# S5 output products of a hybrid decoder layer, regrouped by the shape of the array they use, with the next pair's kernel products moved into the same slot

## The chip, the cores and the metric

The kernel runs on one core of one Trainium2 chip. Times are device microseconds (us) from the start to the end of one execution; lower is better. TensorE is called PE in the profile, VectorE DVE, ScalarE ACT, GpSimd POOL; SP is SyncE, which here only issues DMAs.

## What is computed

One decoder layer over 2048 tokens of width 1024, all in float32. The part that matters here is the S5 branch of the mixer: 32 groups of 16 channels, each with a complex diagonal state of 64.

```python
proj = x @ w_in + b_in
u, ca, cb, gs, gc = jnp.split(proj, SPLITS, axis=-1)
_, _, s_re, s_im = lax.associative_scan(_s5_combine, (a_re, a_im, bu_re, bu_im), axis=1)
y = (jnp.einsum('blgp,ghp->blgh', s_re, c_re) - jnp.einsum('blgp,ghp->blgh', s_im, c_im))
y = jax.nn.gelu(y + d_skip * u)
glu = y @ w_glu + b_glu
s_out = glu[..., :D_MODEL] * jax.nn.sigmoid(glu[..., D_MODEL:])
c_out = _conv_mixer(ca, cb, conv_w, conv_b, ln_c_g, ln_c_b, w_cout, b_cout)
merged = jax.nn.sigmoid(gs) * s_out + jax.nn.sigmoid(gc) * c_out
h = _layer_norm(ALPHA * x + merged @ w_out + b_out, ln1_g, ln1_b)
```

A two-level mixture of 32 SwiGLU experts and a second norm follow; the change does not touch them.

## The kernel before, in words

**The stage.** The large projection runs by column tiles of 128 (`run`, L311), each over four strips of 512 tokens. One strip of one tile is called a slot: 24 products of 128x128 by 128x512 in a split float32 (high by high, high by low, low by high). In the gate tiles 12 to 27 and the two before them, `s5_step` (L729) is called ahead of each slot's products and works on the S5 branch, one pair of groups in four slots, counted from `k = slot - base` with `i, q = divmod(k, 4)`. The state is handled in chunks of 16 tokens: within a chunk a Toeplitz kernel (tile `M0`), from chunk to chunk the scanned state (tile `sx`).

- q = 0: `s5_c(i-1)`, the outputs of the pair before; then, among the vector work of this slot, `s5_a(i)`: twelve DVE products and two copies that make `CA`, `AB` and the block-diagonal `BD`, and the loads of `ut` and `rc` on SP's queue.
- q = 1: `s5_k(i)`: four transposes of `AB` into PSUM (copied by ACT to `BT`), two products of `BD` with `CA` (the chunk kernel, `kt`). DVE finishes `kt` at L651, POOL writes it to DRAM (L652), and SP loads it back as `M0` (L655).
- q = 2: `s5_b(i)`: eight products by 64 columns of `BT`, the two groups by turns, into the two halves of PSUM's partitions.
- q = 3: DVE's rotation and scan of the state, into `sx`.

**The output products.** `s5_c` (L690) makes, for each of the two groups and each half of a chunk, one or two products of `M0` with `ut` (all 128 rows of the array: "whole") and two of `CA` with `sx`, whose 64 rows are the upper or lower half of the array, according to the group ("row halves"). Group 0 comes first, then group 1, so that whole products and row halves alternate: M, CA CA, M M, CA CA, for each group. Each group has its own PSUM tile from the pool `aux`, which has four banks. All these operands are plain float32, and one such product stands in the trace as two passes, each with a weight load.

**What orders the work.** Engines run their own queues in order. Vector work that depends on other engines is put on a list by slot (`later`, `due`, L303 to L309). Work in the background (`bg`: the 31-tap convolution `conv`, L528, then the norm over the channels `norms`, L745, then loads and splits of the output projection's weights) is let out by `fill` (L128) at the end of every slot, as long as an estimated clock of DVE stands 4 us behind an estimated clock of PE (`pe_cost`, L73; `dve_cost`, L65); a step that yields "wait" ends the slot's turn. DVE's clock is never let fall more than 9 us behind. After the gate tiles comes the stage of the S5 output projection (L935 to L968), again 32 slots of 24 products; at its tile 7, strip 0, `drain(1)` (L951) lets out what is left of `norms` at once.

```python
V.t = max(V.t, PE.t + lead - SLOT)      # fill, lead = -4, SLOT = 5
while bg and V.t < PE.t + lead:
```

Of the kernel before, what the change touches and what calls it, by code (L numbers as in the profile page):

```python
# [23 lines left out]
D = 1024  # L24
NS = 4            # strips of 512 tokens
NT = 16           # tiles of 128 tokens
NE = 32
FF = 256
ALPHA = 2.0 ** 0.25
EPS = 1e-5  # L30
CAP = 2048        # rows of the dispatch table for one expert
JB = 4            # blocks of 128 rows laid out for each expert
MAGIC = 12582912.0
# [6 lines left out]

BASE, LEAD, SLOT = 0.10, -4.0, 5.0       # of the estimate of the vector engine's clock

# [12 lines left out]
class Clocked:  # L55
    """An engine whose instructions add their estimated length to a clock."""

# [19 lines left out]
def pe_cost(name, args, kw):  # L77
    if name == "transpose":
        return 0.107
    n = max(_free(args[2]), 64)  # L80
    return n / 2400.0 * (4 if args[2].dtype == F32 else 1)


@with_exitstack
def layer(ctx, tc, a, out, dbg=None):
# [28 lines left out]

    # ---------------------------------------------------------------- constants
    ident = cst.tile([128, 128], F32, name="ident")
# [7 lines left out]

    # vector work that fills the time which the matrix products leave
    bg = []
    ahead = []         # products for that work, at the start of the next slot

# [26 lines left out]

    # ---------------------------------------------------------------- helpers
    def split(hi, lo, src, src2=None):
# [17 lines left out]
    def wload(parts, nk):  # L175
        """parts: [(dram 2-d [rows, 128], first k)]"""
        w = Wt()
        w.nk = nk
        w.raw = wp.tile([128, nk, 128], F32, name="wraw", tag="raw", bufs=1, padded_shape=[128, 8, 128])
        for src, k0 in parts:  # L180
            n = src.shape[0] // 128
            SP.dma_start(w.raw[:, k0:k0 + n, :], src.rearrange("(k p) c -> p k c", p=128))
        return w
# [30 lines left out]

    # ---------------------------------------------------------------- x, transposed and split
    XH = [bigt([128, 8, 512], F32R, f"xh{s}") for s in range(NS)]
# [38 lines left out]
    xfetch(1)  # L255
    TILES = [8, 4, 9, 5, 10, 6, 0, 1, 2, 3, 11, 7] + list(range(12, 28))   # column tiles of w_in, in order
    WL = [(win, m) for m in TILES] + [(wglu, m) for m in range(8)] + [(wcout, m) for m in range(8)]
    WQ = {0: win(TILES[0])}

    def weights(n, s):  # L260
        """the next column tile's weights, while those of tile n are in use"""
        if n + 1 < len(WL):
            if s == 0:
                WQ[n + 1] = WL[n + 1][0](WL[n + 1][1])
            if s == 2:
                wsplit(WQ[n + 1])
# [32 lines left out]

    late = []          # (slot, f): vector work whose operands other engines have made by then  # L300
    slot = [0]
# [9 lines left out]
    def run(n, evac, between=None, first=None):  # L311
        """one column tile of w_in: the products, the next tile's weights, the work of the other engines"""
        w = WQ[n]
# [25 lines left out]

    # ---------------------------------------------------------------- S5: constants  # L340
    sp = spx.enter_context(tc.tile_pool(name="sp", bufs=1))
# [184 lines left out]

    # ---------------------------------------------------------------- convolution branch, u
    def conv(j):  # L528
# [21 lines left out]
    def xnext(s, k):  # L550
        # the next strip of x between the products of this one
        i = 4 * (s + 1) + k // 2
        if i < NT:
            if k % 2 == 0 and i == 4:
                xfetch(4)
                xfetch(5)
            if k % 2 == 0 and i + 2 < NT:
                xfetch(i + 2)
            xturn(i, k % 2)
        if (s, k) == (0, 7):  # L560
            biases()
# [31 lines left out]

    # ---------------------------------------------------------------- S5: one pair of groups at a time
    ss = sax.enter_context(tc.tile_pool(name="ss", bufs=1, side="right"))
    ST = {}

    def s5_a(i):
# [24 lines left out]
        for par in range(2):  # L623
            V.tensor_copy(bd[64 * par:64 * par + 64, :, 16 * par:16 * par + 16],
                          BB[64 * par:64 * par + 64, i])
        ut = ss.tile([128, 2, 2, 128], F32, name="utl", bufs=1)
        SP.dma_start(ut.rearrange("p g k c -> p (g k) c"),
# [62 lines left out]
    def s5_c(i):  # L690
        st = ST.pop(i)
        for par in range(2):
            g = 2 * i + par
            py = paux([128, 2, 128])
            q = slice(64 * par, 64 * par + 64)
            for mt in range(2):
                o = py[:, mt, :]
                PE.matmul(o, st.M0[:, par, 128 * mt:128 * mt + 128], st.ut[:, par, 1, :], start=True, stop=False)
                if mt:
                    PE.matmul(o, st.M0[:, par, 0:128], st.ut[:, par, 0, :], start=False, stop=False)  # L700
                for ri in range(2):
                    PE.matmul(o, st.CA[q, ri, 1 + 8 * mt:9 + 8 * mt, :].rearrange("p d h -> p (d h)"),
                              st.sx[q, ri, 0:128], start=False, stop=ri == 1)
            y1 = ss.tile([128, 2, 128], F32, name="y1", bufs=2)
# [15 lines left out]

    # ---------------------------------------------------------------- gates, with the S5 pairs between
    def g_evac(m):
# [5 lines left out]

    def s5_step():  # L729
        k = slot[0] - base  # L730
        if k == -1:
# [4 lines left out]
        if q == 0:  # L736
            if 1 <= i <= 16:
                s5_c(i - 1)
            if 1 <= i < 16:
                later(0, lambda: s5_a(i))  # L740
        elif i < 16 and q < 3:
            (None, s5_k, s5_b)[q](i)

    # ---------------------------------------------------------------- convolution branch: norm over the channels, silu
    def norms():  # L745
# [123 lines left out]

    # ---------------------------------------------------------------- S5 output, gated  # L870
    gx = ExitStack()
# [14 lines left out]
    def routing_constants():  # L886
        # what routing needs, and a table of dispatch without entries
        G.memset(wr, 0.0)
# [29 lines left out]
    def wo_second():  # L918
        # the output projection's weights, as far as there is room
        wo_load(2, gp, "xr", bufs=2)  # L920
# [48 lines left out]

    # ---------------------------------------------------------------- convolution branch, gated  # L970
    MH = {}
# [7 lines left out]

    # the last column tiles leave the first strips early, whose room the output projection's weights take  # L980
    ENDS = {(7, 1): 4, (6, 2): 5, (6, 3): 6, (7, 2): 7}
# [28 lines left out]

    # ---------------------------------------------------------------- output projection, norm, routing
    dx = ExitStack()
# [94 lines left out]
    def route1(p):  # L1107
# [9 lines left out]
        V.tensor_copy(gi, i8[:, :, 0:1])  # L1117
        # exp(d) = sigmoid(d) / sigmoid(-d)
        sp_, sm_ = small("r_sp", [2, 4]), small("r_sm", [2, 4])
# [60 lines left out]

    # ---------------------------------------------------------------- weights of the experts
    wg, wu, wd = a["w_gate"][0], a["w_up"][0], a["w_down"][0]
# [16 lines left out]

    # the split of one expert's weights, in six steps  # L1200
    def parts(i, k):
# [29 lines left out]
    for p in range(NP):  # L1231
        # the products of pair p, the norm of pair p - 1, the routing of pairs p - 1 and p - 2
        ta, tb = 2 * p, 2 * p + 1
# [69 lines left out]

    # ---------------------------------------------------------------- experts
    ex = ExitStack()
# [88 lines left out]
    def unit(e, b):  # L1394
        """block b of expert e, whose rows are turned; the last block's down projection is left to the next expert"""
        i, j = (e + b) % 2, e % 2
# [41 lines left out]

    # the rows of each expert's last block, and those of the block before it in the order of work
    lst = ep.tile([1, 64], I32, name="lst")  # L1440
# [49 lines left out]

    # rows beyond JB blocks of one expert
    mx = nc.values_load(cnt[0:1, NE:NE + 1], engines=ALL, min_val=0, max_val=S)
# [19 lines left out]

    # ---------------------------------------------------------------- second norm
    fp = ctx.enter_context(tc.tile_pool(name="fp", bufs=1, side="right"))
# [35 lines left out]

    POOL = {1: 1, 2: 3, 3: 1, 4: 3}          # one tile of these groups on the pool engine
    # in PSUM, so that no vector operation reads two tensors of SBUF beside the pool engine
    psx.close()
# [45 lines left out]
    def weave(work, r):  # L1599
        # the root of one group between the passes over others  # L1600
        while work:
# [42 lines left out]
```

## Time and profile before

| | |
|---|---|
| runs shown | 1890.2, 1893.34, 1894.98 us; median 1893.34 |
| profiled execution | span 1892.8 us from the first to the last instruction; no other time of this execution is given, and the median of the runs is 0.5 us above it |
| PE busy | 1755.2 us, 93% |
| DVE busy | 1316.6 us, 70% |
| ACT busy | 684.5 us, 36% |
| POOL busy | 300.9 us, 16% |
| S5 pairs, first to last output product | 285.4 to about 742 us |

A busy PE is not a PE at its best: matmuls overlap one another, and a product that starts late still covers the time. So the distance between the starts of products is read here, not the busy share.

### The profile page before, as it was taken

The numbers are of one execution on the slowest core, as the hardware profiler recorded it, in microseconds if no ns is written. First come the engines' busy times: TensorE is split into PE (matmuls) and PEld (weight loads), VectorE is DVE, ScalarE is ACT, GpSimd is POOL, SyncE is SP. The second block draws the span as 40 slices with busy tenths as digits, with TensorE's granted clock in tenths as the row PEclk, the third lists the DMA queues.
The fourth block names the chain that finished last, engine by engine and source line by source line (L and its number), as shares of the span: only waits on it lengthen the run. The fifth ranks groups of instructions, "written<-read, shape, count | busy, mean of one in ns | idle before, by whom it ended". The sixth has DMA issues, their size and how long they took to land. (4 is left out here: it accounts for less than half of the span.)

```text
span 1892.8 us, 24420 instructions
## 1 busy us (share of the span) xinstructions
PE 1755.2 (93%) x8328; PEld 1413.8 (75%) x8329; DVE 1316.6 (70%) x2388; ACT 684.5 (36%) x1047; POOL 300.9 (16%) x318
## 2 busy tenths in 40 slices
PE   8999999999999999999999999993899999999940
PEld 7888877777777777778888888883688787877730
DVE  5798798788888664664365768786666646657648
ACT  5101212222221234533130122223666656657654
POOL 2000001110101101000000011123223332233215
PEclk9999999999999999999999999996899999999975
DMA  7322422432422432534254333646989968899855
GB/s 221 82 90 61 118 65 75 137 95 75 138 74 92 131 121 91 193 119 156 80 192 128 117 112 114 175 118 191 274 264 287 277 179 249 264 270 291 252 172 230
DMA packets 235908, 301.47 MB, mean 159 GB/s; under 512 B 51230, under 2 KB 181360, under 8 KB 233152
## 3 DMA queue, kind: packets, MB, share of 16 engines
q1 hardware_dynamic: 192336, 212.47, 35.9%
q0 software_dynamic: 23008, 56.06, 10.8%
q10 hardware_dynamic: 20368, 30.42, 4.8%
q8 instruction: 112, 1.84, 0.4%
q14 instruction: 84, 0.69, 0.1%
HBM read 224.35 MB, written 92.31 MB: 167 GB/s over the span
## 5 line engine op out<-in xcount | busy, mean ns | idle before, releaser
L66 PE MATMUL mm<-xh,whi 128*128 128x512 f32 x896 | 362.7, 405 | 0.0
L66 PE MATMUL mm<-xl,whi 128*128 128x512 f32 x896 | 353.2, 394 | 0.0
L66 PE MATMUL mm<-xh,wlo 128*128 128x512 f32 x896 | 352.7, 394 | 0.0
L66 DVE SCALAR_TENSOR_TENSOR cvw<-cvw,cw 128x1024 f32<-128x1024 f32 x240 | 292.0, 1275 | 0.0
L66 PE MATMUL pg<-egu,bh 128*128 128x512 f32 x784 | 251.5, 402 | 5.3 <-ACT edn L1214 5.2
L66 PEld LDWEIGHTS mm<-xh,whi 128*128 128x128 f32 x896 | 168.6, 188 | 47.2 <-issue 8.2
L66 PEld LDWEIGHTS mm<-xh,wlo 128*128 128x128 f32 x896 | 168.5, 188 | 40.5
L66 PEld LDWEIGHTS mm<-xl,whi 128*128 128x128 f32 x896 | 169.0, 189 | 36.1 <-issue 0.7
L66 PEld LDWEIGHTS pg<-egu,bh 128*128 128x128 f32 x784 | 145.1, 190 | 38.2 <-ACT edn L1214 7.3
L66 DVE TENSOR_TENSOR egu<-eraw,egu 128x1024 fp32r<-128x1024 f32 x128 | 151.0, 1221 | 27.3 <-ACT egu L1214 21.5
L66 PE MATMUL mm<-wo,mh 128*128 128x512 f32 x512 | 165.3, 404 | 0.0
L66 PE MATMUL mm<-yt,whi 128*128 128x512 f32 x512 | 163.0, 399 | 2.1 <-ACT yt L848 1.5
L66 PE MATMUL pg<-egu,bl 128*128 128x512 f32 x392 | 155.3, 396 | 0.1
L725 ACT ACTIVATE gt<-mm,cols 128x512 f32<-128x512 f32 x64 | 44.0, 687 | 294.6 <-PE mm L66 282.4
L66 PE MATMUL pd<-edn,hh 128*128 128x512 f32 x392 | 130.1, 414 | 2.0 <-ACT yy L1390 1.1
L1214 ACT ACTIVATE egu<-eraw 128x1024 fp32r<-128x1024 f32 x128 | 124.9, 1059 | 0.4 <-issue 0.4
L66 PEld LDWEIGHTS mm<-yt,whi 128*128 128x128 f32 x512 | 97.1, 190 | 25.7 <-ACT yt L848 1.5
L66 PEld LDWEIGHTS mm<-wo,mh 128*128 128x128 f32 x512 | 97.1, 193 | 21.6
L1175 POOL DMA_INDIRECT td<-r_sd,r_sl x32 | 43.5, 1361 | 395.0 <-DVE r_sl L66 385.0
L66 DVE TENSOR_TENSOR edn<-erd,edn 128x1024 fp32r<-128x1024 f32 x64 | 78.0, 1219 | 40.4 <-ACT edn L1214 40.3
L66 PE MATMUL mm<-wo,ml 128*128 128x512 f32 x256 | 102.7, 401 | 0.0
L66 PE MATMUL mm<-yt,wlo 128*128 128x512 f32 x256 | 101.7, 397 | 0.0
(282 smaller groups left out, 2738.7 us busy)
## 6 DMA issues: line engine op xcount, KB each, us to landing
eraw<-in_w_gate_dram SPq DMA_DIRECT2D x64, 512.0 KB
eraw<-in_w_up_dram SPq DMA_DIRECT2D x64, 512.0 KB
erd<-in_w_down_dram SPq DMA_DIRECT2D x31, 1024.0 KB
gd<-gt ACTq DMA_DIRECT2D x64, 256.0 KB
gl<-gd SPq DMA_DIRECT2D x64, 256.0 KB
wraw<-in_w_in_dram SPq DMA_DIRECT2D x28, 512.0 KB
xt<-in_x_dram SPq DMA_DIRECT2D x16, 512.0 KB
rg<-in_x_dram SPq DMA_DIRECT2D x8, 1024.0 KB
```

The costliest lines, as they stand in the source:

```text
L66: return f(*args, **kw)
L725: A.activation(gt, p, AF.Sigmoid, bias=cols[:, BI + 12 + m:BI + 13 + m])
L1175: d = G.indirect_dma_start(out=td, out_offset=bass.IndirectOffsetOnAxis(ap=sl[:, t, k:k + 1], axis=0), in_=sd[:, t, k, :], in_offset=None)
L1214: A.activation(h, src, AF.Copy)
```

## The change

Besides the hunks below the diff only takes comments out. `pe_cost` counts a float32 product on half of the array at half its length. `s5_c` issues the six whole products of both groups first, then the eight row halves, the groups by turns, each group in its own bank with one `start` and one `stop`. `s5_k(i)` follows `s5_c(i-1)` at q = 0, `s5_a(i+1)` moves to q = 1, and the loads of `ut` and `rc` become `s5_fetch`, due at q = 0 after the DMAs of `s5_k`.

```diff
@@ pe_cost
     n = max(_free(args[2]), 64)
-    return n / 2400.0 * (4 if args[2].dtype == F32 else 1)
+    half = args[2].dtype == F32 and (args[1].shape[0] <= 64 or 32 < _free(args[1]) <= 64)
+    return n / 2400.0 * (4 if args[2].dtype == F32 else 1) * (0.5 if half else 1.0)
@@ s5_a
             V.tensor_copy(bd[64 * par:64 * par + 64, :, 16 * par:16 * par + 16],
                           BB[64 * par:64 * par + 64, i])
+
+    def s5_fetch(i):
+        st = ST[i]
         ut = ss.tile([128, 2, 2, 128], F32, name="utl", bufs=1)
         SP.dma_start(ut.rearrange("p g k c -> p (g k) c"),
@@ s5_c
         st = ST.pop(i)
-        for par in range(2):
+        PY = [paux([128, 2, 128]) for par in range(2)]
+
+        for par, py in enumerate(PY):
+            PE.matmul(py[:, 0, :], st.M0[:, par, 0:128], st.ut[:, par, 1, :], start=True, stop=False)
+            PE.matmul(py[:, 1, :], st.M0[:, par, 128:256], st.ut[:, par, 1, :], start=False, stop=False)
+            PE.matmul(py[:, 1, :], st.M0[:, par, 0:128], st.ut[:, par, 0, :], start=False, stop=False)
+        for mt in range(2):
+            for ri in range(2):
+                for par, py in enumerate(PY):
+                    q = slice(64 * par, 64 * par + 64)
+                    PE.matmul(py[:, mt, :], st.CA[q, ri, 1 + 8 * mt:9 + 8 * mt, :].rearrange("p d h -> p (d h)"),
+                              st.sx[q, ri, 0:128], start=False, stop=mt == 1 and ri == 1)
+        for par, py in enumerate(PY):
             g = 2 * i + par
-            py = paux([128, 2, 128])
-            q = slice(64 * par, 64 * par + 64)
-            for mt in range(2):
-                o = py[:, mt, :]
-                PE.matmul(o, st.M0[:, par, 128 * mt:128 * mt + 128], st.ut[:, par, 1, :], start=True, stop=False)
-                if mt:
-                    PE.matmul(o, st.M0[:, par, 0:128], st.ut[:, par, 0, :], start=False, stop=False)
-                for ri in range(2):
-                    PE.matmul(o, st.CA[q, ri, 1 + 8 * mt:9 + 8 * mt, :].rearrange("p d h -> p (d h)"),
-                              st.sx[q, ri, 0:128], start=False, stop=ri == 1)
@@ s5_step
         if q == 0:
             if 1 <= i <= 16:
                 s5_c(i - 1)
-            if 1 <= i < 16:
-                later(0, lambda: s5_a(i))
-        elif i < 16 and q < 3:
-            (None, s5_k, s5_b)[q](i)
+            if i < 16:
+                s5_k(i)
+                later(0, lambda: s5_fetch(i))
+        elif q == 1 and i < 15:
+            later(0, lambda: s5_a(i + 1))
+        elif q == 2 and i < 16:
+            s5_b(i)
```

## Rows read from the trace of the kernel before

**Rows 1.** Windows: stretch, time, busy PE, PEld, DVE, ACT, POOL, clock, DMA share, GB/s.

```profile
285.00:643.00 358.00, 358.00 (x1782) 280.42 (x1780) 301.17 (x526) 81.51 (x154) 38.26 (x66) 1.00 0.32 101
```

**Rows 2.** Waits of PE from 280 to 760 us: total, times, longest.

```profile
PE aux L66 <- ACT BT L642: 0.7, 2, 0.4
```

**Rows 3.** PE in order of time, output products of one pair (start, us busy).

```profile
463.77 0.39 PE L66 MATMUL mm<-xh,wlo 128*128 128x512 f32 x1
464.00 0.38 PE L66 MATMUL aux<-utl,M 128*128 128x128 f32 x2
464.31 0.71 PE L66 MATMUL aux<-sx,CA 64*128 64x128 f32 x4
464.95 0.71 PE L66 MATMUL aux<-utl,M 128*128 128x128 f32 x4
...
466.23 0.49 PE L66 MATMUL aux<-utl,M 128*128 128x128 f32 x2
466.65 0.71 PE L66 MATMUL aux<-sx,CA 64*128 64x128 f32 x4
...
468.57 0.50 PE L66 MATMUL mm<-xh,whi 128*128 128x512 f32 x1
468.90 0.39 PE L66 MATMUL mm<-xl,whi 128*128 128x512 f32 x1
```

**Rows 4.** PE, `s5_k` one slot later, then `s5_b`, of the next pair.

```profile
474.22 0.60 PE L66 MATMUL aux<-ident,AB 128*128 128x128 f32 x4
474.75 1.05 PE L66 MATMUL aux<-CA,BD 128*32 128x256 f32 x4
475.73 0.50 PE L66 MATMUL mm<-xh,whi 128*128 128x512 f32 x1
...
481.48 1.09 PE L66 MATMUL aux<-utl,BT 128*64 128x128 f32 x16
482.50 0.50 PE L66 MATMUL mm<-xh,whi 128*128 128x512 f32 x1
```

**Rows 5.** SP's queue: the loads of `M0` after `kt`.

```profile
478.66 1.23 SPq L655 DMA_DIRECT2D M<-kd  x2
```

**Rows 6.** ACT in the same slots.

```profile
468.68 0.38 ACT L706 ACTIVATE y<-aux 128x256 f32<-128x256 f32 x1 [1.41 <-PE aux L66]
...
469.51 1.04 ACT L158 ACTIVATE whi<-wraw 128x1024 fp32r<-128x1024 f32 x1
...
475.51 0.60 ACT L642 ACTIVATE BT<-aux 128x512 f32<-128x512 f32 x1 [0.40 <-ACT gt L725]
476.00 0.35 ACT L648 ACTIVATE kt<-aux 32x240 f32<-32x240 f32 x1
```

**Rows 7.** DVE: rotation and scan of the state, first and last group, then the weights' low part.

```profile
459.39 0.73 DVE L66 TENSOR_TENSOR e<-aux,rc 128x256 f32<-128x256 f32 x2
...
462.13 0.49 DVE L66 TENSOR_TENSOR sx<-e,e 128x128 f32<-128x128 f32 x2
...
470.58 1.23 DVE L66 TENSOR_TENSOR wlo<-wraw,whi 128x1024 fp32r<-128x1024 f32 x1 [1.50 <-ACT whi L158]
```

**Rows 8.** DVE and PE, the first pair: `s5_a(0)` from first to last, transposes of `s5_k(0)`.

```profile
255.66 0.43 DVE L66 TENSOR_TENSOR q<-PWr,CTr 128x272 f32<-128x272 f32 x1
...
260.65 0.36 DVE L66 COPY BD<-BB 64x32 f32<-64x32 f32 x2
...
265.85 0.60 PE L66 MATMUL aux<-ident,AB 128*128 128x128 f32 x4
```

**Rows 9.** DVE: last convolution taps, last norm step, evacuation of the drain's slot.

```profile
630.81 4.86 DVE L66 SCALAR_TENSOR_TENSOR cvw<-cvw,cw 128x1024 f32<-128x1024 f32 x4
...
859.32 2.49 DVE L66 TENSOR_TENSOR nw<-nw 128x512 f32<-128x512 f32 x4
...
950.15 0.75 DVE L66 SCALAR_TENSOR_TENSOR sb<-mm,cols,sb 128x512 f32<-128x512 f32 x1 [4.09 <-PE mm L66]
```

**Rows 10.** PE in the output projection's stage: a norm product that waits for DVE.

```profile
829.98 1.12 PE L66 MATMUL aux<-nw,onesm 128*128 128x512 f32 x2 [1.70 <-DVE nw L66]
```

## The prediction

> **What bounds the kernel now.** The page and the windows come first: in the S5 stretch PE is busy the whole time at the full granted clock, 1.00 (2.4 GHz), DVE 84% of it, ACT 23% [rows 1]. The waits say the same from the other side: of 480 us PE waits 0.7 us for another engine [rows 2]. So this stage lasts as long as PE's own list of products, and what is left is to read what each product costs in the order of time. That view is the one that matters, because a busy share hides it: a product that starts late counts as busy too.
>
> In the order of time the output products of one pair take from 464.00 to 468.57 [rows 3]. Compare two groups of one kind. Four passes that follow a change between whole products and row halves take 0.64 us (464.31 to 464.95), two take 0.42 (466.23 to 466.65). The difference is two passes, so **a pass is 0.11 us**, and what is left of either, 0.64 - 0.44, is **0.20 us for each change of shape**. The last change, back to the projection, shows half of its 0.20 inside the group before and half in the first product after it, which takes 0.33 (468.57 to 468.90) where an undisturbed one takes 0.23 (463.77 to 464.00). From the projection into the first whole product nothing is lost: that step is the same 0.23. The sum closes: 28 passes x 0.11 + 8 changes x 0.20 = 4.68 us, against 4.57 + 0.10 = 4.67 read. A third of the output products is changing shape.
>
> **The change part by part.** *Grouping.* Six whole products of both groups stand first, then eight row halves: two changes are left of eight. 6 x 0.20 = 1.20 us less a pair, 19.2 us for 16 pairs. This needs nothing but the two prices just read.
>
> *Row halves by turns.* Upper and lower rows alternate, each group in its own bank. Whether two passes then run at once no row shows, for before has row halves of one group only in succession, at 0.11 each. The bounds are the nearest rows. At one end they run one after the other, 16 x 0.11 = 1.76 us, no gain. At the other end they behave as the column halves of `s5_b`, also float32 and also by turns: 16 passes fill 1.02 us up to the next product [rows 4], of which 0.10 is the change back, so 0.115 for two. Then 8 x 0.11 = 0.88 us, and 0.88 less a pair, 14.1 us in all. I take the second: same pass, same alternation, only the other axis of the array. So 12 x 0.11 + 0.20 + 0.88 + 0.20 = 2.60 us replaces 4.68: 2.08 x 16 = **33.3 us**; without overlap 19.2.
>
> The Trainium skill (TensorE: Matmul & The Clock Gate, Part 3, measured speedup) gives 3.07 times for four row tiles where four would be ideal. If two suffered by the same factor, an estimate from that page, the halves would take 1.15 us instead of 0.88, and the gain would be about 29 us instead of 33; the column halves in the trace show no such loss.
>
> *`s5_k` at q = 0.* Four transposes and two products with their changes, 474.22 to 475.73 and 0.10 after [rows 4], 1.6 us, cost the same in either slot: they entered without loss from the projection, and now enter by the change that I counted as the way out of the row halves. Zero. Its two PSUM tiles and the two of the outputs now fill all four banks in one slot. A norm product let out in that slot must wait until ACT has copied `BT`; in its old place this wait was 0.4 us at most [rows 2], and most norm products will fall after the S5 stage (below). Between -0.7 and +2 us; I take 0. For the first pair `s5_k(0)` comes one slot sooner. Its slot begins 24 products before 265.85, at 260.3, and `s5_a(0)` ends on DVE at 261.0 [rows 8]: **0.6 us lost**, once.
>
> *DMAs.* The chain `kt`, write to DRAM, two loads of `M0` begins one slot sooner, and `ut` and `rc` now stand behind it on SP's queue. The second `M0` load was through 3.5 us after ACT's `kt` (479.9 after 476.35) [rows 5, 6]. Let T0 be the start of the pair's first whole product: `kt` will be ready at T0 + 5.2 (next paragraph), so `ut` is issued at about T0 + 9; `s5_b` wants it two slots on, at T0 + 2.5 + 1.6 + 2 x 5.6 = 15.3. SP's next own load, a weight tile, is issued at q = 2 as well. Hidden by 6 us; were it not, each us late would cost 16. POOL issues the same writes, one of them a slot sooner: zero.
>
> *DVE.* `s5_a` moves from q = 0 to q = 1, and `kt` becomes DVE's first work at q = 0. Behind the waiting `kt` stand the weights' low part, all background work of the slot and, three slots on, `sx`, for which PE waits. When is `kt` there? The outputs end at T0 + 2.4; ACT takes 0.3 to start, four activations at 0.41 (two from 468.68 to 469.51), `BT` 0.49, `kt` 0.35 [rows 6]: T0 + 5.2. The copy of the weights follows, 1.04, and DVE starts on their low part at T0 + 6.2, as before (470.58 is T0 + 6.6) [rows 7]. From there to the end of `sx`: low part 1.15, `s5_a` 5.35 [rows 8], two steps for the last outputs 0.7 each, rotation and scan 3.23 (459.39 to 462.62), and the convolution taps of three slots at 1.215 [rows 7, 9]. The taps come from the planner's arithmetic in the code: a pair's PE estimate falls from 26.4 to 24.7 (half products at half price), fixed vector work is 10.5, and at q = 0 the floor in `fill` forgives another 1.6 because the slot got longer and its vector work shorter; 12.6 are left, at 1.23 a tap 10, one or two of them after `sx`. With nine before it `sx` ends at T0 + 28.2. PE's next row halves start at 96 x 0.232 + 2.6 + 1.6 + 1.3 = 27.8 plus 1.5 for the whole products ahead of them: 29.3. So `sx` has **1 us of slack**, 0 with ten taps; it has 1.7 in the pair shown (462.62 against 464.31). I allow 1 us in all for pairs that miss.
>
> *Background work.* The same arithmetic gives the kernel before 15.9 / 1.23 = 12.9 taps a pair. Its last tap ends at 635.7 [rows 9], 12.8 pairs of 29.8 us behind 255.7; at 10.2 a pair the same taps take 16 pairs. So the convolution ends about 13 slots later (11 to 14 with a tap more or less), and the norm with it. The last norm step stands now at 859.3, 16 slots before the drain's slot, which is evacuated at 950.15 [rows 9]. So it ends 2 to 5 slots ahead of the drain: still covered. But strips of the norm that ran in the S5 stage move into the shorter slots of the next stage, where the product at a strip's border waited 1.7 us for DVE [rows 10]; two more such borders come there, with the refill 1.9 each: **+3.8 us**.
>
> **The sum.** -33.3 + 0.6 + 1 + 3.8 = -27.9 us against the profiled execution's 1892.8; that span lies 0.5 below the median of the runs, 1893.34, against which the forecast is made: **1865.4 us**. The stages that follow run in the same order from where this one ends, none of them is tied to a fixed time, so the gain should reach the end.
>
> **The rivals.** *The row halves do not overlap* (the change does half of what it says): grouping alone, 19.2 less the same 5.4, 1879.5 us. For it: not one row shows two row groups at once. Against it: column halves do it in this very stage. By the Trainium skill (TensorEngine Tiling (Array Packing), Gotcha 1) row tiles cannot use one PSUM bank at once; the change gives each group its own.
>
> *`sx` is late.* If DVE gets 11 taps in, or ACT's chain at q = 0 is a us longer, PE waits 1 to 1.5 us a pair while the convolution lasts, some 14 pairs: 14 to 21 us back, 1879 to 1886. For it: a slack of 1 us. Against it: if DVE lags, it also waits less for `kt`, where it stands idle some 4 us a pair by the schedule above.
>
> *Slower: the norm is not done at the drain.* Then PE stands at `drain(1)` while a strip's vector work goes by alone, some 20 us (14 of DVE, the rest ACT and the copy to DRAM; an estimate from its seven steps at 2 to 2.8 us [rows 9]). It decides the sign from one and a half strips left, when the convolution falls 12 slots further behind than I work out; with two strips left 1865 + 40 = 1905. Against it: a margin of 2 to 5 slots, and the arithmetic of the planner is exact up to where a slot begins.
>
> **How the numbers follow.** A measurement of this kernel tells about 0.3% from no change, 5.7 us. Forecast 0.65; no overlap 0.14; `sx` late 0.12; norm undone 0.04; 0.05 for what I do not see, of either sign. The first three all lie more than 5.7 us below: faster 0.92, same 0.03, slower 0.05. The range goes down to the full 33.3 with none of the losses and 2 us of scatter between runs, 1858, and up over the rival without overlap to 1881.
>
> **What would show it.** In the changed kernel a pair's output products should stand as one run of 12 whole passes and one of 16 row halves, the second taking 0.9 to 1.1 us up to the next transposes; 1.8 means no overlap. A pair should take 27.8 us instead of 29.9. PE's waits should stay near zero in the stage; a wait of `sx,CA` for DVE `sx` is the second rival, one of the projection or a norm product around the drain the third. The taps should end 11 to 14 slots later. The prediction is wrong if the stage shortens by less than 25 us, or if it does and the end does not follow.

## The result, and the profile after

The changed kernel takes 1861.47 us (median of 4 runs, 1857.16 to 1862.73), where the kernel before took 1894.16 beside it (4 runs): a ratio of 0.9822, 95% interval 0.9809 to 0.9836. That is 32.7 us less by the medians and 33.5 by the spans of the profiled executions. The forecast was 27.9 less, 1865.4 us, with a range from 1858 to 1881.

The page after, its first lines:

```profile
span 1859.3 us, 24405 instructions
...
PE 1720.4 (93%) x8328; PEld 1388.4 (75%) x8329; DVE 1317.2 (71%) x2388; ACT 683.3 (37%) x1047; POOL 301.3 (16%) x318
```

PE's busy time fell by 34.8 us, and its share stayed at 93%. DVE, ACT and POOL moved by 1.2 us at most. The windows after, with the columns of [rows 1], for the same stretch of the S5 stage and for the output projection's stage behind it:

```profile
285.00:643.00 358.00, 358.00 (x1912) 282.95 (x1911) 279.56 (x513) 86.85 (x166) 40.99 (x70) 1.00 0.33 104
742.00:934.00 192.00, 189.36 (x830) 151.58 (x831) 123.18 (x210) 81.84 (x106) 3.25 (x11) 1.00 0.43 136
```

In the same 358 us PE gets through 1912 matmul records instead of 1782 [rows 1], 7% more. It is busy for all of it in both kernels, so the busy share alone would have shown nothing. PE's waits from 285 to 742 us have no line at all after the change ([rows 2] had 0.7 us).

PE in order of time, after (start, us busy): the first pair's transposes, then the outputs of the pair of [rows 3] with the next pair's kernel products, the start of the pair after it, then the first product of the next stage and a norm product there:

```profile
260.44 0.38 PE L66 MATMUL aux<-ident,AB 128*128 128x128 f32 x2
260.98 0.44 PE L66 MATMUL aux<-ident,AB 128*128 128x128 f32 x2 [0.16 <-DVE AB L66]
261.35 1.05 PE L66 MATMUL aux<-CA,BD 128*32 128x256 f32 x4
...
452.42 0.39 PE L66 MATMUL mm<-xh,wlo 128*128 128x512 f32 x1
452.65 1.50 PE L66 MATMUL aux<-utl,M 128*128 128x128 f32 x12
454.08 1.16 PE L66 MATMUL aux<-sx,CA 64*128 64x128 f32 x16
455.17 0.66 PE L66 MATMUL aux<-ident,AB 128*128 128x128 f32 x4
455.76 1.05 PE L66 MATMUL aux<-CA,BD 128*32 128x256 f32 x4
456.74 0.50 PE L66 MATMUL mm<-xh,whi 128*128 128x512 f32 x1
...
480.44 1.50 PE L66 MATMUL aux<-utl,M 128*128 128x128 f32 x12
...
742.09 0.50 PE L66 MATMUL mm<-yt,whi 128*128 128x512 f32 x1 [1.46 <-ACT yt L858]
...
875.48 1.10 PE L66 MATMUL aux<-nw,onesm 128*128 128x512 f32 x2 [0.97 <-DVE nw L66]
```

The outputs are one run of 12 whole passes and one of 16 row halves. From 452.65 to 455.17 they take 2.52 us. The four transposes behind them take 0.59 (455.17 to 455.76) where they took 0.53 before [rows 4]; that puts 0.06 of the last change there, so 2.58 us replaces 4.67. The row halves take 1.09 up to the transposes. Less 0.20 for the change into them, this is 0.89 for 16 passes: **two at a time, at 0.11 for both**.

Where the 33.5 us came from, by the starts of stages in the two traces (us):

| start of | before | after | difference |
|---|---|---|---|
| first output product | 285.40 | 285.93 | +0.5 |
| output projection (`mm<-yt`) | 779.68 | 742.09 | -37.6 |
| the stage after that (`mm<-ct`) | 966.61 | 934.01 | -32.6 |
| experts (`pg`) | 1316.50 | 1282.77 | -33.7 |
| end of the span | 1892.8 | 1859.3 | -33.5 |

A pair takes 27.79 us instead of 29.77 (452.65 to the next pair's 480.44; 464.00 to 493.77 before): 1.98 x 16 = 31.7. The last three of the fifteen intervals of before were longer, 30.6, 32.1 and 32.0 us, because norm products stood between them; with another 1.0 us behind the last pair that is 6.4 us more. PE before, in order of time: the start of the pair after that of [rows 3], then the norm products in the first two of the longer intervals (642.60 to 673.23 to 705.33):

```profile
493.77 0.38 PE L66 MATMUL aux<-utl,M 128*128 128x128 f32 x2
...
661.10 1.13 PE L66 MATMUL aux<-nw,onesm 128*128 128x512 f32 x2
...
677.80 1.05 PE L66 MATMUL aux<-onesm,nw 128*128 128x1 f32 x8
...
686.34 1.16 PE L66 MATMUL aux<-ident,cn_rs 128*128 128x128 f32 x8 [0.36 <-ACT BT L642]
```

Of the four strips of the norm, three had their `nw` products in the S5 stage before; after, one has them there and three in the next stage.

All of this left the stage: 38.1 us. The next stage took it up and grew from 186.9 to 191.9 us. PE's waits there, from 742 to 940 us (total, times, longest):

```profile
PE mm L66 <- ACT yt L858: 1.5, 1, 1.5
PE aux L66 <- DVE nw L66: 1.2, 2, 1.0
PE aux L66 <- DVE cn_rs L66: 0.6, 1, 0.6
PE mm L66 <- DVE yt L66: 0.6, 1, 0.6
```

The two lines of the norm, `nw` and `cn_rs`, come to 1.8 us; before there was one of 1.7 [rows 10].

DVE and then ACT around the same pair, with the taps up to the next `sx`, and DVE at the end of the background work:

```profile
452.31 0.50 DVE L66 TENSOR_TENSOR sx<-e,e 128x128 f32<-128x128 f32 x2
...
457.76 0.22 DVE L66 SCALAR_TENSOR_TENSOR kt<-dmask,dsk,aux 32x16 f32<-32x16 f32 x1 [3.76 <-ACT kt L652]
458.71 1.22 DVE L66 TENSOR_TENSOR wlo<-wraw,whi 128x1024 fp32r<-128x1024 f32 x1 [0.73 <-ACT whi L159]
459.85 6.06 DVE L66 SCALAR_TENSOR_TENSOR cvw<-cvw,cw 128x1024 f32<-128x1024 f32 x5
...
472.55 4.87 DVE L66 SCALAR_TENSOR_TENSOR cvw<-cvw,cw 128x1024 f32<-128x1024 f32 x4
...
480.09 0.49 DVE L66 TENSOR_TENSOR sx<-e,e 128x128 f32<-128x128 f32 x2
...
709.21 1.28 DVE L66 SCALAR_TENSOR_TENSOR cvw<-cvw,cw 128x1024 f32<-128x1024 f32 x1
...
905.93 2.49 DVE L66 TENSOR_TENSOR nw<-nw 128x512 f32<-128x512 f32 x4
...
917.55 0.75 DVE L66 SCALAR_TENSOR_TENSOR sb<-mm,cols,sb 128x512 f32<-128x512 f32 x1 [4.09 <-PE mm L66]
```

```profile
455.27 0.38 ACT L712 ACTIVATE y<-aux 128x256 f32<-128x256 f32 x1 [1.74 <-PE aux L66]
...
456.91 0.58 ACT L646 ACTIVATE BT<-aux 128x512 f32<-128x512 f32 x1
457.39 0.34 ACT L652 ACTIVATE kt<-aux 32x240 f32<-32x240 f32 x1
```

`sx` ends at 452.81, 1.27 us before the row halves at 454.08 ask for it. Nine taps stand between `kt` and the next `sx`, and a tenth behind it. DVE stands idle 3.76 us in front of `kt`, and PE waits for neither. The last tap is now at 709.21, and the last norm step ends at 908.42, 9 us ahead of the evacuation of the drain's slot at 917.55.

### The profile page after: what moved, and what is told of

It reads as the page before. It is cut to its first block, busy times and chain, and to the rows that moved or that the text cites. A ratio compares the mean times of both kernels' runs of the same rounds, so it can differ in the third digit from the quotient of the medians.

```text
span 1859.3 us, 24405 instructions
## 1 busy us (share of the span) xinstructions
PE 1720.4 (93%) x8328; PEld 1388.4 (75%) x8329; DVE 1317.2 (71%) x2388; ACT 683.3 (37%) x1047; POOL 301.3 (16%) x318
```

## The experiments

The theory: the time came from PE's own list of products, by six changes of shape less a pair and by row halves of two groups that run at once; the move of `s5_k` and the new estimate cost and bring nothing. Rivals: the order of the halves brings nothing by itself, a part of the gain comes from the move, or from the different pace of the background work. The ratios are against the kernel before; that of the change itself is 0.9822 (0.9809 to 0.9836). Each edit is to the changed kernel, but for the move alone, which is made to the kernel before.

**The row halves of one group after the other's.**

```diff
-        for mt in range(2):
-            for ri in range(2):
-                for par, py in enumerate(PY):
+        for par, py in enumerate(PY):
+            for mt in range(2):
+                for ri in range(2):
```

> The changed kernel, but the row halves of group 0 all stand before those of group 1, so that no two neighbours use different rows. The whole products still stand first: two changes of shape a pair, as in the changed kernel. Theory (upper and lower rows run at once): the 16 half passes take 1.76 us instead of 0.89, a pair 28.66 us instead of 27.79, and the kernel is 14 us slower than the changed one, about 1875 us. Rival (the overlap does nothing, the grouping alone made the gain): no difference, 1861 us, and the half passes of the changed kernel must be as short for another reason.

Measured: 1866.35 us, ratio 0.9871 (0.9848 to 0.9895); a pair took 28.23 us, half way between the two expectations. PE in order of time:

```profile
455.87 1.71 PE L66 MATMUL aux<-sx,CA 64*128 64x128 f32 x16
457.51 0.66 PE L66 MATMUL aux<-ident,AB 128*128 128x128 f32 x4
```

The halves take 1.64 instead of 1.09, where one by one they would take 16 x 0.11 + 0.20 = 1.96. The starts of the single passes, in us after 455, say why:

```
0.873 1.087 1.198 1.310 1.422 | 1.427 1.533 1.641 1.645 1.752 1.757 1.864 1.976 2.087 2.199 2.311
```

Up to the bar the passes come one by one, 0.11 apart (0.21 for the first, with a part of the change in it). The pass behind the bar starts 5 ns after the fifth, so it can only be one of the other rows, the second group's first; of the first group's eight passes, which all stand before it in the program, three are still to come. ACT bears it out: its first work on the first group's outputs starts at 457.06, as the pass at 1.757 ends (0.272 long), and counted in steps of 0.11 from 0.873 that pass is the first group's eighth.

```profile
457.06 0.38 ACT L712 ACTIVATE y<-aux 128x256 f32<-128x256 f32 x1 [1.74 <-PE aux L66]
```

Three times two passes start within 5 ns of each other (1.422, 1.641, 1.752), which makes 13 steps of 16 passes: 13 x 0.11 + 0.20 = 1.63. So **the overlap is real**, and without turns a part of it is lost: 0.44 us a pair, 7 us in the stage. The halves alone lose 0.55; the other 0.11 comes back in the two slots behind them, where the projection's products start 0.231 us apart and not 0.233. But neither theory had it right: neighbours in the list are not needed, since PE starts a pass ahead of three others.

**Turns of two.** This came later, to see how far PE looks.

```diff
-            for ri in range(2):
-                for par, py in enumerate(PY):
+            for par, py in enumerate(PY):
+                for ri in range(2):
```

> The changed kernel with the row halves by turns of two products (four passes of one group, then four of the other) instead of one by one. In the run with whole groups in succession three passes of the one group stood behind the first of the other, so PE started that one ahead of them. Theory (PE looks a few passes ahead for the other half of the array): nearly full overlap, at most 0.25 us a pair more than one by one, 27.8 to 28.05 us. Rival (only neighbours overlap): four passes in a row hold the other group up each time, 28.4 us a pair or more.

Measured: 1860.12 us, ratio 0.9819 (0.9803 to 0.9835), a pair 27.79 us. PE in order of time:

```profile
454.22 1.26 PE L66 MATMUL aux<-sx,CA 64*128 64x128 f32 x16
455.42 0.33 PE L66 MATMUL aux<-ident,AB 128*128 128x128 f32 x1
```

The halves take 1.20, one pass (0.11) more than by turns of one. By the single starts, passes start two together seven times, and two passes start alone; a product is two passes, so here PE already sets the first pass of the list beside the fifth. The pair does not show the 0.11, as the projection products of the next two slots start 0.231 us apart and not 0.233; why was not looked into.

**Two more changes of shape.** Four of the six whole products, those of the second half of the chunk, stand between the row halves of the first and of the second; nothing else differs.

```diff
-            PE.matmul(py[:, 1, :], st.M0[:, par, 128:256], st.ut[:, par, 1, :], start=False, stop=False)
-            PE.matmul(py[:, 1, :], st.M0[:, par, 0:128], st.ut[:, par, 0, :], start=False, stop=False)
         for mt in range(2):
+            if mt:
+                for par, py in enumerate(PY):
+                    PE.matmul(py[:, 1, :], st.M0[:, par, 128:256], st.ut[:, par, 1, :], start=False, stop=False)
+                    PE.matmul(py[:, 1, :], st.M0[:, par, 0:128], st.ut[:, par, 0, :], start=False, stop=False)
```

> The changed kernel, but the whole products of the second half of the chunk stand between the row halves of the first and of the second: four changes of shape a pair instead of two, the halves still by turns. Theory (a change costs 0.20 us, and PE is the bound): 0.40 us more a pair, 6.4 us in all, about 1868 us, pair 28.19 us. Rival (the changes cost little, because the weights of the next shape can be loaded ahead while halves alternate): under 2 us.

Measured: 1866.85 us, ratio 0.9864 (0.9846 to 0.9881); a pair took 28.18 us, 0.39 more. PE in order of time:

```profile
454.24 0.61 PE L66 MATMUL aux<-utl,M 128*128 128x128 f32 x4
454.77 0.72 PE L66 MATMUL aux<-sx,CA 64*128 64x128 f32 x8
455.42 1.16 PE L66 MATMUL aux<-utl,M 128*128 128x128 f32 x8
456.51 0.71 PE L66 MATMUL aux<-sx,CA 64*128 64x128 f32 x8
457.15 0.66 PE L66 MATMUL aux<-ident,AB 128*128 128x128 f32 x4
```

Eight passes of row halves take 0.65 (454.77 to 455.42), which is 4 x 0.11 and one change of 0.20. The price of a change holds: 0.39 / 2 = 0.195 us.

**The move undone, and the move alone.**

```diff
+            if 1 <= i < 16:
+                later(0, lambda: s5_a(i))
             if i < 16:
-                s5_k(i)
                 later(0, lambda: s5_fetch(i))
-        elif q == 1 and i < 15:
-            later(0, lambda: s5_a(i + 1))
+        elif q == 1 and i < 16:
+            s5_k(i)
```

> The changed kernel, but the kernel products are back in the slot after the outputs and the vector work for them in the outputs' slot, as before the change. Theory (the move is worth nothing on PE): 1861 us within 3, pair 27.8 us; DVE waits for kt about 1.5 us a pair instead of 3.8 and more convolution taps are let out in a pair, so the norm ends earlier. Rival (the move is part of the gain, since PE found M0 or the state late in the old order): 5 us or more slower, with waits of PE for sx or M0.

```diff
-            if 1 <= i < 16:
-                later(0, lambda: s5_a(i))
-        elif i < 16 and q < 3:
-            (None, s5_k, s5_b)[q](i)
+            if i < 16:
+                s5_k(i)
+                later(0, lambda: s5_fetch(i))
+        elif q == 1 and i < 15:
+            later(0, lambda: s5_a(i + 1))
+        elif q == 2 and i < 16:
+            s5_b(i)
```

> The kernel before with the move of the kernel products and of the vector work alone; order of the output products and the estimates of PE as before. Theory: no gain, 1894 us within 3, pair 29.8 us. Rival (the move is part of the gain): 1889 us or less.

Measured: undone, 1863.28 us, ratio 0.9842 (0.9827 to 0.9856), a pair 27.72 us; alone, 1893.48 us, ratio 0.9994 (0.9981 to 1.0007), a pair 29.83 against 29.77. PE's waits from 285 to 742 us, with the move undone and then with the move alone:

```profile
PE aux L66 <- ACT BT L646: 0.4, 1, 0.4
```

```profile
PE aux L66 <- DMA utl<-ud: 1.1, 1, 1.1
```

With the move undone PE goes straight from the row halves to the projection, and the halves take the same 1.09 us.

```profile
452.94 1.16 PE L66 MATMUL aux<-sx,CA 64*128 64x128 f32 x16
454.03 0.50 PE L66 MATMUL mm<-xh,whi 128*128 128x512 f32 x1
```

**The move brings nothing**: the whole times do not tell it from no change, and the pair is 0.07 and 0.06 us longer with it, 1 us in 16 pairs. The change out of the halves is paid to the transposes or to the projection, as the prediction had it.

**The full estimate for row and column halves.** The planner counts the half products at their whole price again, so that it lets out more background work a pair.

```diff
-    return n / 2400.0 * (4 if args[2].dtype == F32 else 1) * (0.5 if half else 1.0)
+    return n / 2400.0 * (4 if args[2].dtype == F32 else 1) * 1.0
```

> The changed kernel with the old estimate of PE's products (half products counted in full). Theory (the estimate only moves background work about): more convolution taps a pair (11 by the planner's arithmetic instead of 10), the norm ends four slots or more earlier, the pair stays at 27.8 us and the time at 1861 us within 3. Rival (the fuller schedule makes DVE late for sx, and the lower estimate is what keeps the gain): PE waits for sx, 5 us or more slower.

Measured: 1861.87 us, ratio 0.9832 (0.9814 to 0.9849). Eleven taps a pair instead of ten, 2.58 us of idle time before `kt` instead of 3.76, and the last norm strip written at 885.97 instead of 908.72. The pair is the same, 27.79 us. Background work that comes 23 us sooner brings nothing here, since it was in time as it was.

**Row halves first, whole products after them**: the same two changes, but `sx` is wanted 1.43 us sooner (452.65 to 454.08).

```diff
-        for par, py in enumerate(PY):
-            PE.matmul(py[:, 0, :], st.M0[:, par, 0:128], st.ut[:, par, 1, :], start=True, stop=False)
...
         for mt in range(2):
...
-                              st.sx[q, ri, 0:128], start=False, stop=mt == 1 and ri == 1)
+                              st.sx[q, ri, 0:128], start=mt == 0 and ri == 0, stop=False)
+        for par, py in enumerate(PY):
+            PE.matmul(py[:, 0, :], st.M0[:, par, 0:128], st.ut[:, par, 1, :], start=False, stop=False)
...
```

> The changed kernel with the row halves ahead of the whole products; same products, same two changes of shape. PE then wants sx 1.4 us sooner. Theory (sx has 1.28 us of slack in the changed kernel, no more): PE waits 0.1 to 0.3 us for sx in the pairs in which the convolution is let out, 28.0 us a pair, 2 to 4 us slower in all. Rival (DVE has room, the whole products first are not needed): no wait, 27.8 us a pair.

Measured: 1859.57 us, ratio 0.9812 (0.9799 to 0.9826), a pair 27.75 us, and no wait of PE for `sx`. One pair took 29.02, for here too PE waited once for the load of `ut`. PE, DVE and that wait:

```profile
451.43 1.16 PE L66 MATMUL aux<-sx,CA 64*128 64x128 f32 x16
```

```profile
450.56 0.49 DVE L66 TENSOR_TENSOR sx<-e,e 128x128 f32<-128x128 f32 x2
```

```profile
PE aux L66 <- DMA utl<-ud: 1.2, 1, 1.2
```

`sx` ends at 451.05, 0.38 before it is wanted; a wait of 0.1 to 0.3 us was expected, so this expectation fell. It left out that the first group's whole products now end ahead of the second's: ACT starts on the first group sooner, and DVE has `kt` 2.03 us after the transposes begin instead of 2.59 (457.76 - 455.17). What DVE has to do until the next `sx` then starts sooner as well.

**`BD` in a wider buffer.** One buffer of 160 columns, read at 0 and at 32, lets the two kernel products use all 128 columns of the array; the products in rows 32 and up are not read.

```diff
-    BD = [sp.tile([128, 2, 32], F32, name=f"BD{i}") for i in range(2)]
+    BD = [sp.tile([128, 160], F32, name="BD0")] * 2
...
-        pk = paux([32, 256])
-        PE.matmul(pk, st.bd[:, 0, :], st.CA[:, 0, 0:16, :].rearrange("p d h -> p (d h)"), start=True, stop=False)
-        PE.matmul(pk, st.bd[:, 1, :], st.CA[:, 1, 0:16, :].rearrange("p d h -> p (d h)"), start=False, stop=True)
+        pk = paux([128, 256])
+        PE.matmul(pk, st.bd[:, 0:128], st.CA[:, 0, 0:16, :].rearrange("p d h -> p (d h)"), start=True, stop=False)
+        PE.matmul(pk, st.bd[:, 32:160], st.CA[:, 1, 0:16, :].rearrange("p d h -> p (d h)"), start=False, stop=True)
```

> The changed kernel with the block-diagonal weights of the kernel products widened with zeros to 128 columns (one buffer of 160 columns), so that they too use the whole array: the change of shape into them and the one out of them fall away. Theory (0.20 us a change): 0.40 us less a pair, 27.4 us, 6.4 us in all, 1855 us. Rival (only the change between row halves and whole products costs, or the wider weights cost as much): 27.8 us a pair, 1861 us.

Measured: 1857.68 us, ratio 0.9804 (0.979 to 0.9817); a pair took 27.48 us, 0.31 less. PE in order of time:

```profile
429.40 0.66 PE L66 MATMUL aux<-ident,AB 128*128 128x128 f32 x4
429.89 1.03 PE L66 MATMUL aux<-CA,BD 128*128 128x256 f32 x4
430.57 0.58 PE L66 MATMUL mm<-xh,whi 128*128 128x512 f32 x1
430.99 0.40 PE L66 MATMUL mm<-xl,whi 128*128 128x512 f32 x1
```

From the transposes to the `BD` products it is 0.49 instead of 0.59, and from these to the second projection product 1.10 instead of 1.31 (455.76 to 457.07). So the change into 32 columns cost 0.10, the change out 0.21: 0.31 and not 0.40.

**Both once more**, side by side, to settle the order of the two.

> The changed kernel itself, beside the next one on the same chip. Every theory: 1861 us, 0.982 of the kernel before, pair 27.8 us.

> The widened block-diagonal weights again, now beside the changed kernel on the same chip. In its first run a pair took 27.48 us instead of 27.79: 0.31 us less, not 0.40, because the change into a weight block of 32 columns had cost 0.12 and not 0.20. Theory (PE is the bound, the gain reaches the end): 5 us faster than the changed kernel, 1856 to 1857 us. Rival (the first run's 1857.7 was scatter): no difference from the changed kernel.

(The rows above give 0.10 for the change into 32 columns, not 0.12.) Measured: the changed kernel 1863.47 us, ratio 0.9829 (0.9816 to 0.9843); the wide `BD` 1858.85 us, ratio 0.9806 (0.9792 to 0.9819). The wide `BD` had the lower median both times, by 3.8 us the first time (0.9804 against 0.9822, each beside its own runs of the kernel before) and by 4.6 the second; 16 x 0.31 would give 5.0. But the two intervals overlap each time. Its gain is plain in the stage, which takes 451.4 and 451.5 us from the first output product to the output projection, where the changed kernel takes 456.2 in both of its executions. The stages around it scatter by as much: the first output product stands at 285.3 to 289.5 in these four, and the expert stage takes 575.6 to 582.5. So the whole time only suggests the lead.

## Why the prediction was right, and where it was off

- **The price of a pass and of a change: right.** 0.11 and 0.20 us, read from groups of different length, gave 2.60 us for a pair's outputs; 2.58 was measured. Putting two changes back cost 0.195 each.
- **The row halves run at once: right.** Before had no row of it, and the column halves stood for it. Expected 0.88, measured 0.89; the rival without overlap would have shown 1.76. By the Trainium skill (TensorE: Matmul & The Clock Gate, Part 3, measured speedup) an estimate from 3.07 times for four row tiles was 1.15; two row groups here lose nothing, and the trace decides. By the Trainium skill (TensorE: Matmul & The Clock Gate, Part 3, The mechanism) matmuls start and end in the order of the program. The run with one group after the other differs from it, with a start ahead of three passes (1.427 against 1.533, 1.645 and 1.757), and again the trace decides.
- **The pair: nearly.** 1.98 us less instead of 2.08, so 31.7 instead of 33.3. (The prediction's 27.8 for a pair hit 27.79 partly by luck: it started from 29.9, where the rows have 29.77.) The outputs account for 2.09 (4.67 - 2.58). The other 0.1 lies in the projection, whose products start 0.233 us apart in the two slots after the outputs instead of 0.231. The turns of two, and one group after the other, had 0.231 there. The cause stays open.
- **The first pair: right in kind, a little smaller.** PE waits for `AB` there: its four transposes take 0.91 us (260.44 to 261.35) where they took 0.53 in [rows 4], so 0.4 and not 0.6 is lost. The 0.5 of the table holds scatter from ahead of the stage too: in the second execution of the changed kernel the same transposes took 0.91 as well, and the first output product stood at 285.27.
- **`sx`: right that it does not decide; the 1 us allowed for it was not lost.** `kt` and the low part came as worked out: 457.76 and 458.71 are 5.1 and 6.1 us after the pair's first product, against 5.2 and 6.2. With nine taps before it, as forecast, `sx` ends 27.9 us after that product (480.58), against 28.2, and the slack is 1.3 us against 1. DVE's idle time before `kt`, some 4 us by the forecast, was 3.76.
- **The background work: right in time, wrong in price. This is the step that failed.** The taps end 14 slots later (11 to 14 forecast), the last norm step two slots ahead of the drain (2 to 5 forecast), and the norm did move into the next stage, which grew by 5.0 us. But 3.8 us were added for it with nothing taken away. The same norm products had lengthened the last three pairs of before and the end of the stage by 6.4 us, and all of that left. The net is -1.4, so the term missed by 5.2 us. Nearly all of the difference between 27.9 and 33.5 is this: the prediction counted what arrived in the next stage and not what left this one. (The other terms missed by 1.6 us one way and 2.0 the other, and all but cancel.) Nor did the waits grow: 1.8 us at the norm's borders, where 1.7 and two more of 1.9 had been expected.
- **The move and the new estimate: right, nothing; but the margin of `ut` was misread.** That they bring nothing is shown by undoing each and by the move alone. The 6 us by which `ut` was to be hidden run from its issue to its use, without the load itself. In most pairs of the changed kernel the issue stands 6.8 us ahead of the product that wants it, where it stood 13.4 ahead before. SP's issue and then that product, after:

```profile
461.35 0.46 SPq L631 DMA_DIRECT2D utl<-ud  x1
...
468.13 1.09 PE L66 MATMUL aux<-utl,BT 128*64 128x128 f32 x16
```

In two of the ten executions with the move PE waited for it in one pair, 1.1 us with the move alone and 1.2 with the halves first. There the load took 4.9 and 5.0 us from its issue to PE's start, so some 2 us is what is left in most pairs.

The measured sum: -31.7 for the pairs, +0.5 for the first, -1.4 for the norm and -0.9 in the stages behind, together -33.5. The last of these can't be told from scatter: it lies in the stage ahead of the experts (`mm<-ct` to `pg`), which took 349.9 us before, 348.8 after and 350.8 in the second execution of the changed kernel. The expert stage took 576.5 and 579.0 in those two.

Not tried: both groups' halves in one PSUM bank. By the Trainium skill (TensorEngine Tiling (Array Packing), Gotcha 1) different row tiles cannot access the same bank at once. No run here shows what it costs.

## What to carry to other kernels

Where PE is busy all the time, compare groups of the same product but of different length in order of time: what does not scale with their number is the price of changing shape, and products sorted by shape save it. Two row groups with a bank each run at once, best when their passes take turns, and a narrow weight block padded to the array's full width saves its changes. When background work moves to a later stage, take its cost out of the stage that it leaves before adding it to the one that it enters.

## What the runs showed of the hardware that was not expected

PE starts a pass of the other row half ahead of three that stand before it in the program (1.427 beside 1.422 in the listing of starts above), so that even one group's row halves after the other's took 1.64 us and not 1.96. That engines run their queues in order, as the text ahead has it, does not hold for PE's passes. And changes are not all of one price: into a block of 32 weight columns it is 0.10 us, out of it 0.21, where a change between whole products and row halves is 0.20.
